# A fp32 encoder block on one core: 256-byte place of the split weights, and the down projection's operands made in steps

## The chip, the cores and the metric

The kernel runs on one core of one Trainium2 chip. The metric is the device time of one execution in microseconds (us). TensorE (PE) multiplies, VectorE (DVE) and ScalarE (ACT) work on tiles in SBUF and PSUM, GpSimd (POOL) issues some transfers, and SyncE (SP) issues most of them.

## The reference

One layer of a bidirectional encoder: 512 tokens, model width 2048, float32 throughout.

```python
h = rmsnorm(x, attn_norm_g);  z = h @ w_in          # [q latent | kv latent | rope key | conv B | C | H]
attn   = attention(8 heads, 128 + 64 rope, no mask)  # from the latents
y_conv = gate_b * conv3_centred(gate_c * sc_h, sc_conv_w)
x = x + concat(rmsnorm(attn), rmsnorm(y_conv)) @ w_o
h = rmsnorm(x, ffn_norm_g)
u = conv3_centred(h @ w_ffn_up, ffn_conv_w) + ffn_conv_b   # 2048 -> 2 x 5632
g, val = split(u);  x = x + (silu(g) * val) @ w_ffn_down   # 5632 -> 2048
return rmsnorm(x, final_norm_g)
```

## The kernel before

**How float32 is kept.** Every float32 operand is split into two tiles of a shorter type: `hi` is a copy by ACT (`split`, L234), `lo` is the difference `src - hi` by DVE (L231, the body of `tt`). A product is then three matmuls, `whi*xhi`, `whi*xlo`, `wlo*xhi` (`mm3` and `product`). Weights come in units of 128x1024 float32 (`raw`, 8 buffers, pool `wraw`, loaded by SP at L261), and each unit is split into a `hi` and a `lo` tile (3 buffers each, pool `wsp`, 4096 bytes in a partition). All other tiles (activations, their halves, sums) are `t` tiles of 128x512 (pool `tp`, 80 buffers, 2048 bytes in a partition); all `t` tiles have the same place modulo 256 bytes. The pools lie one behind the other in the order in which they are made: `cpool`, `tp`, `sp`, `wraw`, `wsp`. In the program as built the `t` tiles begin at 160 modulo 256 bytes and the `hi` and `lo` tiles at 96, which is 192 past the `t` tiles.

**The stages.** Input projections, attention, output projection, the first six tiles of the up projection (`up_plain`) multiply with 512 moving columns at L244 (`mm`). From the seventh of the 44 up tiles on (`up_seven`), and in the down projection (`down_seven`), a 2x2 block product is made by seven products instead of eight (`seven`): 24 matmuls of 256 moving columns for each product (`product`, L880), in the order f1, g7, h6, f2, h5, g4, h3 of PSUM bank and product. Copies by ACT at L936, L957, L969 and L931 take the banks over. One up tile is 7 products, one block of the down projection also 7 (168 matmuls). The down projection runs over five chunks of eight up tiles and in each over four blocks `m`; a last chunk of four tiles runs with plain products of 256 columns at L244 (`last_half`).

**Operands of the down projection.** `gated` saves each activation tile to DRAM through POOL (L782). `sums_of(c, i)` brings two of them back through SP (`restore`, L787) and makes of them the operands of the seven products (`make_operands`): on DVE two differences of 256 columns, two `scalar_tensor_tensor` of 256 columns (L845, L846), one `lo` of 256 and three of 512; on ACT one cast of 256 and three of 512. `fetch_xr` brings 16 tiles of x back in 32 transfers (L1005).

**What sets the order.** The kernel writes a list of items, one for each product; `run` loads weights three or four items ahead, splits them two or three ahead, issues an item's matmuls, and then its `posts` (functions with a lag in items). Over that a scheduler of the framework reorders instructions across engines when the program is built. Each engine then runs its own queue in order, and waits where an input or a buffer isn't free. `sums_of` of chunk 0 stands whole at four of the last up tile's seven items; that of chunk c+1 stands whole on the third item of each block of chunk c.

Of the kernel before, what the change touches and what calls it, by code (L numbers as in the profile page):

```python
# [47 lines left out]
KD = D // P  # L51
# [9 lines left out]
NF = FF // P  # L61
EPS = 1e-6
SCALE = float(1.0 / np.sqrt(np.float32(NOPE + ROPE)))
UW = 1024
NT = 80
NPLAIN = 6
ORDER = [0, 1, 2, 3, 4]
EARLY = ()
AHEAD = 4
HT = T // 2  # L70
FILL = 3
# [100 lines left out]
def encoder_block(ctx: ExitStack, tc: tile.TileContext, gx, wall, vecs, rot, out):  # L172
    nc = tc.nc
    cpool = ctx.enter_context(tc.tile_pool(name="cpool", bufs=1))
    tp = ctx.enter_context(tc.tile_pool(name="tp", bufs=NT))
    sp = ctx.enter_context(tc.tile_pool(name="sp", bufs=2))
    wraw = ctx.enter_context(tc.tile_pool(name="wraw", bufs=8))
    wsp = ctx.enter_context(tc.tile_pool(name="wsp", bufs=3))
    dram = ctx.enter_context(tc.tile_pool(name="dram", bufs=1, space=bass.MemoryType.DRAM))
# [2 lines left out]
    def tile_r():  # L182
        return tp.tile([P, T], F32R, tag="t", name="t")

    def pair():
        return tile_r(), tile_r()

    def ztile():
        return tp.tile([P, T], F32, tag="t", name="t")
# [13 lines left out]
    first = cpool.tile([P, KD + T], F32, name="first")  # L203
    ga = first[:, :KD]
    vec = cpool.tile([P, NVEC], F32, name="vec")
    nvec = cpool.tile([P, 3 * NF], F32, name="nvec")
    cs = []


# [53 lines left out]

    def split_unit(key, part, raw):
        n = part.stop - part.start
        hi = wsp.tile([P, UW], F32R, tag="hi", name="hi")
        lo = wsp.tile([P, UW], F32R, tag="lo", name="lo")
        if key[0] == "kr":

            r = raw.rearrange("p (k c) -> p k c", c=ROPE)  # L270
            w = [z.rearrange("p (k c) -> p k c", c=P) for z in (hi, lo)]
            for j in range(2):
                split((w[j][:, :, :ROPE], w[j][:, :, ROPE:]), r[:, 8 * j:8 * j + 8, :])
            return w
# [48 lines left out]
    items = []  # L323
# [221 lines left out]
    v, qr, qk, pr = {}, {}, {}, {}  # L545
# [227 lines left out]
    def half(t, i):  # L773
        return t[:, i * HT:(i + 1) * HT]
# [3 lines left out]
    def save(name, src):  # L778

        saved[name] = [(dram.tile([P, T], F32, name=f"{name[0]}{name[1]}_{i}"), t.dtype) for i, t in enumerate(src)]  # L780
        for (o, _), t in zip(saved[name], src):
            nc.gpsimd.dma_start(o, t.bitcast(F32))  # L782

    def restore(name):
        ts = [tp.tile([P, T], dt, tag="t", name="t") for _, dt in saved[name]]
        for o, (d, _) in zip(ts, saved[name]):
            nc.sync.dma_start(o.bitcast(F32), d)  # L787
        return ts
# [6 lines left out]
        if s == 0:  # L795
            nc.scalar.activation(u, u, AF.Silu)

    kept = {}

    def gated(us, f):  # L800
        tt(us[1], us[0], us[1], ALU.mult)
        if f // 8 in EARLY:
            kept[f] = us[1]
            if f % 2:
                save(("sums", f // 2), make_operands(kept.pop(f - 1), kept.pop(f)))
            return
        if f < starts[last]:
            save(("act", f), [us[1]])
            return
        a = pair()  # L810
        split(a, us[1])
        save(("act", f), a)
# [19 lines left out]
    operands = []  # L832

    def normed_operands(i):
        (a,), (b,) = restore(("xr", 2 * i)), restore(("xr", 2 * i + 1))
        for k, t in ((2 * i, a), (2 * i + 1, b)):
            nc.vector.scalar_tensor_tensor(out=t, in0=t, scalar=col("ffn_g", k), in1=rx.r, op0=ALU.mult, op1=ALU.mult)
        operands.append(views(make_operands(a, b)))

    def make_operands(a, b):  # L840

        u, v = ztile(), ztile()
        tt(half(u, 0), half(a, 0), half(a, 1), ALU.subtract)
        tt(half(u, 1), half(b, 1), half(a, 1), ALU.subtract)
        nc.vector.scalar_tensor_tensor(out=half(v, 0), in0=half(a, 0), scalar=-1.0, in1=half(u, 1), op0=ALU.mult, op1=ALU.subtract)  # L845
        nc.vector.scalar_tensor_tensor(out=half(v, 1), in0=half(v, 0), scalar=-1.0, in1=half(b, 0), op0=ALU.mult, op1=ALU.subtract)  # L846
        one = tile_r()
        split((half(one, 0), half(one, 1)), half(a, 0))
        ts = [one]
        for src in (u, v, b):  # L850
            p = pair()
            split(p, src)
            ts += p
        return ts

    def views(ts):

        got = {1: (half(ts[0], 0), half(ts[0], 1))}
        for i, names in enumerate(((5, 7), (6, 4), (2, 3))):
            for j, q in enumerate(names):  # L860
                got[q] = half(ts[1 + 2 * i], j), half(ts[2 + 2 * i], j)
        return got

    banks = []
# [18 lines left out]
    def seven(index, units, posts, ops, wide=HT, lean=False):  # L883


        z, raw = {}, {}
# [6 lines left out]
            return f  # L893

        def parts(src):
            hi = wsp.tile([P, UW], F32R, tag="hi", name="hi")
            lo = wsp.tile([P, UW], F32R, tag="lo", name="lo")
            split((hi, lo), src)
            return hi, lo

# [41 lines left out]
        kept, kept2 = [() if a in posts else (a,) for a in ("s7", "u2")]  # L942
# [35 lines left out]
    starts = [sum(CHUNKS[:i]) for i in range(len(CHUNKS))]  # L978
    last = len(CHUNKS) - 1
# [10 lines left out]
    items.extend(plain)  # L990
    for f in range(NPLAIN, NF):
        items.extend(up_seven(f))


    acts, xt, sums = {}, {}, {}
# [9 lines left out]
                    nc.sync.dma_start(half(xt[m, a, h], e), half(saved[("xr", 4 * m + 2 * e + a)][0][0], h))  # L1005

    def sums_of(c, i):
        f = starts[c] + 2 * i
        if c in EARLY:
            ts = restore(("sums", f // 2))  # L1010
        else:
            (a,), (b,) = (restore(("act", f + j)) for j in range(2))
            ts = make_operands(a, b)
        sums.setdefault(c, []).append(views(ts))

    def down_seven(c, m):
        def onto(a, h, op):
# [7 lines left out]
        return seven(m, units, posts, sums.setdefault(c, []), T, True)  # L1025

    at = len(items) - 7
    for i, j in enumerate((0, 2, 4, 5)):
        items[at + j].posts.append((0, lambda i=i: sums_of(ORDER[0], i)))
    for m in range(KD // 4):  # L1030
        items[at + (5, 6, 6, 6)[m]].posts.append((0, lambda m=m: fetch_xr(m)))
    for c, after in zip(ORDER, ORDER[1:] + [None]):
        for m in range(KD // 4):
            its = down_seven(c, m)
            if after is not None:
                its[2].posts.append((0, lambda c=after, m=m: sums_of(c, m)))
            items.extend(its)

    def fetch(f):
# [99 lines left out]
```

## Time and profile before

| | us |
|---|---|
| median of 3 runs | 2034.42 |
| lowest, highest | 2032.77, 2034.82 |
| profiled execution, its own time | 2035.79 |
| span of its instructions | 2034.0 |
| PE busy | 1997.3 (98%) |
| DVE busy | 1542.0 (76%) |
| ACT busy | 977.4 (48%) |

The mean granted clock of PE is 0.992. In a row of a group stand line, engine, operation, output and inputs, shapes, count, then busy time and the mean of one in ns. Matmuls overlap (each starts before the one ahead has drained), so that the mean of one is longer than the distance from start to start; the pace of a stream is read from starts, or from a count in a window. In a row of the timeline stand start, duration of the row, engine, line, operation, and in brackets the idle time ahead of it with what ended it.

### The profile page before, as it was taken

The numbers are of one execution on the slowest core, as the hardware profiler recorded it, in microseconds if no ns is written. First come the engines' busy times: TensorE is split into PE (matmuls) and PEld (weight loads), VectorE is DVE, ScalarE is ACT, GpSimd is POOL, SyncE is SP. The second block draws the span as 40 slices with busy tenths as digits, with TensorE's granted clock in tenths as the row PEclk, the third lists the DMA queues.
The fourth block names the chain that finished last, engine by engine and source line by source line (L and its number), as shares of the span: only waits on it lengthen the run. The fifth ranks groups of instructions, "written<-read, shape, count | busy, mean of one in ns | idle before, by whom it ended". The sixth has DMA issues, their size and how long they took to land.

```text
span 2034.0 us, 33864 instructions
## 1 busy us (share of the span) xinstructions
PE 1997.3 (98%) x13826; PEld 1848.2 (91%) x13826; DVE 1542.0 (76%) x1893; ACT 977.4 (48%) x1358; POOL 209.6 (10%) x204
## 2 busy tenths in 40 slices
PE   8999999999999999999999999999997999999997
PEld 7888888888888888999999999999997999999997
DVE  7375877664556587788888888888887998987776
ACT  6253534433224344555555555555565554444454
POOL 5001232310001000000000000000010001000000
PEclk9999999999999999999999999999998999999998
DMA  7322222222444344445545545545557776677642
GB/s 259 100 86 78 78 78 73 73 91 95 133 138 140 130 156 138 136 134 152 171 136 151 170 137 150 172 138 148 170 143 219 225 197 172 186 187 199 179 116 83
DMA packets 94155, 290.78 MB, mean 143 GB/s; under 512 B 10672, under 2 KB 18992, under 8 KB 94000
## 3 DMA queue, kind: packets, MB, share of 16 engines
q1 hardware_dynamic: 77648, 230.95, 33.9%
q0 software_dynamic: 16352, 57.68, 13.7%
q8 instruction: 108, 1.77, 0.4%
q14 instruction: 47, 0.39, 0.1%
HBM read 267.62 MB, written 20.97 MB: 142 GB/s over the span
## 4 chain that ended last, share of the span: by engine, by line
PE 90%; DVE 4%; DMA 2%; issue 1%; ACT 0%; SPq 0%; DVEq 0%; ACTq 0%
PE ps L880 50%; PE ps L244 41%; DVE t L231 2%; DMA t<-act 2%; DVE lo L231 2%; DVE raw L231 0%; ACT hi L234 0%; DVE t L846 0%; SPq L787 0%; DVE t L845 0%; SPq L261 0%; DVE t L489 0%; DVEq L1134 0%; ACT ps L931 0%; ACT t L349 0%
## 5 line engine op out<-in xcount | busy, mean ns | idle before, releaser
L880 PE MATMUL ps<-t,hi 128*128 128x256 f32 x6496 | 1118.5, 278 | 17.7 <-ACT hi L234 7.2
L880 PEld LDWEIGHTS ps<-t,hi 128*128 128x128 f32 x6496 | 978.1, 188 | 20.3 <-DVE t L231 8.0
L234 ACT CAST hi<-raw 128x1024 fp32r<-128x1024 f32 (+1 forms) x544 | 568.3, 1047 | 702.9 <-PE ps L244 242.3
L880 PE MATMUL ps<-t,lo 128*128 128x256 f32 x3248 | 884.4, 278 | 1.9 <-DVE lo L231 1.9
L231 DVE TENSOR_TENSOR lo<-raw,hi 128x1024 fp32r<-128x1024 f32 (+1 forms) x543 | 668.4, 1232 | 198.4 <-ACT hi L234 188.3
L244 PE MATMUL ps<-t,hi 128*128 128x512 f32 x2096 | 654.3, 394 | 4.4 <-ACT t L239 3.5
L880 PEld LDWEIGHTS ps<-t,lo 128*128 128x128 f32 x3248 | 602.8, 188 | 2.6 <-DVE lo L231 2.5
L244 PEld LDWEIGHTS ps<-t,hi 128*128 128x128 f32 x2096 | 394.3, 189 | 92.0 <-ACT t L239 4.2
L244 PE MATMUL ps<-t,lo 128*128 128x512 f32 x1056 | 411.4, 392 | 0.0
L231 DVE TENSOR_TENSOR t<-ps,t 128x512 f32<-128x512 f32 (+3 forms) x255 | 143.0, 575 | 152.6 <-PE ps L244 99.8
L231 DVE TENSOR_TENSOR t<-t 128x512 fp32r<-128x512 f32 (+4 forms) x356 | 223.1, 645 | 34.2 <-DMA t<-act 13.2
L244 PEld LDWEIGHTS ps<-t,lo 128*128 128x128 f32 x1056 | 198.9, 188 | 45.0 <-issue 0.5
L231 DVE TENSOR_TENSOR raw<-raw 128x1024 f32<-128x1024 f32 x154 | 187.8, 1219 | 0.5
L244 PE MATMUL ps<-t 128*128 128x256 f32 (+1 forms) x642 | 108.6, 326 | 0.0
L234 ACT CAST t<-t 128x512 fp32r<-128x512 f32 (+2 forms) x149 | 81.3, 577 | 48.8 <-DVE t L231 25.1
L244 PEld LDWEIGHTS ps<-t 128*128 128x128 f32 x642 | 95.1, 190 | 10.3
L231 DVE TENSOR_TENSOR t<-t,ps 128x512 f32<-128x512 f32 x128 | 86.7, 683 | 21.1 <-PE ps L880 19.7
L782 POOL DMA_DIRECT2D act<-t x48 | 27.4, 570 | 694.4 <-DVE t L231 658.9
L231 POOL TENSOR_TENSOR t<-t 128x512 f32<-128x512 f32 x39 | 64.1, 1645 | 72.3 <-DVE t L231 40.5
L904 POOL DMA_DIRECT2D raw<-wall x58 | 50.3, 868 | 163.6 <-ACT t L936 69.4
L910 POOL DMA_DIRECT2D raw<-wall x20 | 17.1, 854 | 316.8 <-DVE lo L231 215.5
L343 ACT ACTIVATE t<-l 128x512 f32<-128x512 f32 x44 | 27.5, 626 | 45.7 <-DVE l L231 45.5
(81 smaller groups left out, 825.3 us busy)
## 6 DMA issues: line engine op xcount, KB each, us to landing
raw<-wall SPq DMA_DIRECT2D x372, 512.0 KB, 4.3
raw<-wall POOLq DMA_DIRECT2D x78, 512.0 KB, 7.4
act<-t POOLq DMA_DIRECT2D x48, 256.0 KB, 2.5
t<-act SPq DMA_DIRECT2D x48, 256.0 KB, 5.1
t<-gx SPq DMA_DIRECT2D x16, 256.0 KB, 3.8
xr<-l POOLq DMA_DIRECT2D x16, 256.0 KB, 2.4
t<-xr SPq DMA_DIRECT2D x16, 256.0 KB, 4.0
t<-xr SPq DMA_DIRECT2D x32, 128.0 KB, 3.9
```

What stands on the lines that cost most here:

```text
L231: (eng or nc.vector).tensor_tensor(out=o, in0=a, in1=b, op=op)
L234: nc.scalar.copy(out=dst[0], in_=src)
L244: nc.tensor.matmul(ps, lhsT=w, rhs=x, start=start, stop=stop)
L343: nc.scalar.activation(sq, src, AF.Square)
L782: nc.gpsimd.dma_start(o, t.bitcast(F32))
L880: nc.tensor.matmul(half(ps, e), lhsT=w[a][:, c:c + P], rhs=ops[k][q][b], start=start and e == k == i == 0, stop=k == n - 1 and i == 2, ski ...
L904: nc.gpsimd.dma_start(raw["a21"], wall[UIDX[units["a22"]]], accum_op=ALU.add)
L910: nc.gpsimd.dma_start(raw["s"], wall[UIDX[units["a12"]]], accum_op=ALU.add)
```

## The change

Two things, beside the removal of code that does nothing here (`ORDER`, `EARLY`, `kept`, `views`).

The first is **addresses**. The `hi` and `lo` buffers grow by 64 floats (`ROOM`). Weights for 512 columns (`split_unit`) use the start of the buffer; weights for 256 columns (`parts` in `seven`) start 48 floats, which is 192 bytes, behind it. The pool `sp` is made ahead of `tp`, and the small table `nvec` lies in a part of `first` that the input's first tile no longer needs, and not in a tile of its own. In the program as built the `t` tiles and the `hi` and `lo` buffers then all begin at 64 modulo 256 bytes: 512-column weights lie 0 past the tiles (before 192), 256-column weights 192 past them (as before). The one product that uses `t` tiles as weights and `hi`, `lo` as 256 moving columns (`values` in the attention, 192 matmuls) goes from a distance of 64 to 0.

The second is **steps**. `sums_of` now returns five functions: a fetch of two tiles, and four steps of the making of operands. For chunk 0 they are posted from eight items ahead of the last up tile's first on, to its last; for later chunks on the items 0, 2, 3, 4, 5 of a block.

```diff
+ROOM = 64
+SHIFT = 48
...
+    sp = ctx.enter_context(tc.tile_pool(name="sp", bufs=2))
     tp = ctx.enter_context(tc.tile_pool(name="tp", bufs=NT))
-    sp = ctx.enter_context(tc.tile_pool(name="sp", bufs=2))
...
-    nvec = cpool.tile([P, 3 * NF], F32, name="nvec")
+    nvec = first[:, KD:KD + 3 * NF]
...
     def split_unit(key, part, raw):
-        hi = wsp.tile([P, UW], F32R, tag="hi", name="hi")
-        lo = wsp.tile([P, UW], F32R, tag="lo", name="lo")
+        hi, lo = (wsp.tile([P, UW + ROOM], F32R, tag=a, name=a)[:, :UW] for a in ("hi", "lo"))
...
         def parts(src):
-            hi = wsp.tile([P, UW], F32R, tag="hi", name="hi")
-            lo = wsp.tile([P, UW], F32R, tag="lo", name="lo")
+            hi, lo = (wsp.tile([P, UW + ROOM], F32R, tag=a, name=a)[:, SHIFT:SHIFT + UW] for a in ("hi", "lo"))
...
+    def operand_steps(a, b, got):
+        z = {}
+        def parts(src, *names):
+            p = pair()
+            split(p, src)
+            for j, q in enumerate(names):
+                got[q] = half(p[0], j), half(p[1], j)
+        def first():
+            z["u"], one = ztile(), tile_r()
+            tt(half(z["u"], 0), half(a(), 0), half(a(), 1), ALU.subtract)
+            tt(half(z["u"], 1), half(b(), 1), half(a(), 1), ALU.subtract)
+            got[1] = half(one, 0), half(one, 1)
+            split(got[1], half(a(), 0))
+        def second():
+            v = z["v"] = ztile()
+            nc.vector.scalar_tensor_tensor(out=half(v, 0), in0=half(a(), 0), scalar=-1.0, in1=half(z["u"], 1), op0=ALU.mult, op1=ALU.subtract)
+            nc.vector.scalar_tensor_tensor(out=half(v, 1), in0=half(v, 0), scalar=-1.0, in1=half(b(), 0), op0=ALU.mult, op1=ALU.subtract)
+            parts(z["u"], 5, 7)
+        return first, second, lambda: parts(z["v"], 6, 4), lambda: parts(b(), 2, 3)
...
     def sums_of(c, i):
-        f = starts[c] + 2 * i
-        if c in EARLY:
-            ts = restore(("sums", f // 2))
-        else:
-            (a,), (b,) = (restore(("act", f + j)) for j in range(2))
-            ts = make_operands(a, b)
-        sums.setdefault(c, []).append(views(ts))
+        z, f = {}, starts[c] + 2 * i
+        got = {}
+        sums.setdefault(c, []).append(got)
+        def fetch2():
+            for j in range(2):
+                (z[j],) = restore(("act", f + j))
+        return fetch2, *operand_steps(lambda: z[0], lambda: z[1], got)
...
-    for i, j in enumerate((0, 2, 4, 5)):
-        items[at + j].posts.append((0, lambda i=i: sums_of(ORDER[0], i)))
+    for i, when in enumerate(((-8, -6, -5, -4, -3), (-1, 1, 1, 2, 3), (1, 4, 4, 5, 5), (3, 4, 5, 6, 6))):
+        for j, step in zip(when, sums_of(0, i)):
+            items[at + j].posts.append((0, step))
...
-            if after is not None:
-                its[2].posts.append((0, lambda c=after, m=m: sums_of(c, m)))
+            if c + 1 < last:
+                for j, step in zip((0, 2, 3, 4, 5), sums_of(c + 1, m)):
+                    its[j].posts.append((0, step))
```

In the program as built the queues differ only from the second to last up tile to the fourth block of the down projection; in later blocks single rows of 128x256 change places. Three places there follow.

**SP's queue at the end of the up projection.** `raw` are weight loads, `act` the fetches of activations in pairs. Before:

```order
L261 DMA raw<-wall 128x1024 x151
L787 DMA t<-act_0_5498 128x512
L787 DMA t<-act_0_5690 128x512
L261 DMA raw<-wall 128x1024 x2
L787 DMA t<-act_0_5882 128x512
L787 DMA t<-act_0_6047 128x512
L261 DMA raw<-wall 128x1024
L787 DMA t<-act_0_6311 128x512
L787 DMA t<-act_0_6389 128x512
```

and after:

```order
L264 DMA raw<-wall 128x1024 x147
L789 DMA t<-act_0_5497 128x512
L789 DMA t<-act_0_5689 128x512
L264 DMA raw<-wall 128x1024 x3
L789 DMA t<-act_0_5881 128x512
L789 DMA t<-act_0_6046 128x512
L264 DMA raw<-wall 128x1024 x2
L789 DMA t<-act_0_6310 128x512
L789 DMA t<-act_0_6388 128x512
```

The first pair stands four weight loads earlier, the second three, the third two; the fourth pair, not shown, stands one earlier.

**DVE's queue in the second to last up tile.** Rows of 128x1024 are weights (`lo`, or sums of `raw`), rows of 128x512 belong to the saved activation, rows of 128x256 to the operands. Before:

```order
L231 TENSOR_TENSOR t_14746<-t_14780,t_14746 128x512
L231 TENSOR_TENSOR lo_14854<-raw_14576,hi_14853 128x1024
L231 TENSOR_TENSOR raw_14948<-raw_14814,raw_14816 128x1024
L231 TENSOR_TENSOR t_14820<-t_14746,t_14819 128x512
L231 TENSOR_TENSOR lo_14886<-raw_14617,hi_14885 128x1024
L231 TENSOR_TENSOR lo_14919<-raw_14708,hi_14918 128x1024
```

and after:

```order
L234 TENSOR_TENSOR t_14745<-t_14783,t_14745 128x512
L234 TENSOR_TENSOR lo_14863<-raw_14575,hi_14862 128x1024
L234 TENSOR_TENSOR raw_14972<-raw_14817,raw_14819 128x1024
L234 TENSOR_TENSOR t_14823<-t_14745,t_14822 128x512
L234 TENSOR_TENSOR t_14856<-t_14773 128x256
L234 TENSOR_TENSOR t_14856<-t_14775,t_14773 128x256
L234 TENSOR_TENSOR lo_14902<-raw_14616,hi_14901 128x1024
L234 TENSOR_TENSOR t_14857<-t_14773,t_14857 128x256
L855 SCALAR_TENSOR_TENSOR t_14894<-t_14773,t_14856 128x256
L234 TENSOR_TENSOR lo_14939<-raw_14707,hi_14938 128x1024
```

The first pair's differences now stand ahead of a weight's `lo`. On PE the product of `lo_14902` now goes ahead of that of `lo_14863`; in before the product of `lo_14854` went ahead of that of `lo_14886`.

**ACT's queue ahead of the last up tile's seventh product.** `hi` are weights, `t<-t` casts of operands, `t<-ps` the copy that empties the PSUM bank of the sixth product's place for the next one. Before:

```order
L234 CAST hi_15208<-raw_14948 128x1024
L234 CAST t_15067<-t_15055 128x512
L234 CAST t_15071<-t_15052 128x512
L234 CAST t_15084<-t_14986 128x512
L936 COPY t_15124<-ps_15093 128x256
L234 CAST t_15160<-t_15150 128x256
```

and after:

```order
L237 CAST hi_15215<-raw_14972 128x1024
L237 CAST t_15130<-t_15121 128x512
L938 COPY t_15144<-ps_15096 128x256
L237 CAST t_15170<-t_15127 128x512
L938 COPY t_15180<-ps_6303 128x256
```

One cast stands between the weight's `hi` and the copy where three stood.

## Rows read from the trace of the kernel before

**Rows 1.** The page: busy share of PE, and the chain by line.

```profile
PE 1997.3 (98%) x13826; PEld 1848.2 (91%) x13826; DVE 1542.0 (76%) x1893; ACT 977.4 (48%) x1358; POOL 209.6 (10%) x204
PE ps L880 50%; PE ps L244 41%; DVE t L231 2%; DMA t<-act 2%; DVE lo L231 2%; DVE raw L231 0%; ACT hi L234 0%; DVE t L846 0%; SPq L787 0%; DVE t L845 0%; SPq L261 0%; DVE t L489 0%; DVEq L1134 0%; ACT ps L931 0%; ACT t L349 0%
```

**Rows 2.** The page's groups of matmuls: shapes, count, busy us, mean ns.

```profile
L880 PE MATMUL ps<-t,hi 128*128 128x256 f32 x6496 | 1118.5, 278 | 17.7 <-ACT hi L234 7.2
...
L880 PE MATMUL ps<-t,lo 128*128 128x256 f32 x3248 | 884.4, 278 | 1.9 <-DVE lo L231 1.9
...
L244 PE MATMUL ps<-t,hi 128*128 128x512 f32 x2096 | 654.3, 394 | 4.4 <-ACT t L239 3.5
...
L244 PE MATMUL ps<-t,lo 128*128 128x512 f32 x1056 | 411.4, 392 | 0.0
```

**Rows 3.** Timeline of PE, 190 to 216 us: split weights, attention, split weights.

```profile
189.69 0.39 PE L244 MATMUL ps<-t,lo 128*128 128x512 f32 x1
...
197.47 7.41 PE L244 MATMUL ps<-t 128*128 128x512 f32 x32
204.72 0.62 PE L244 MATMUL ps<-t,hi 128*128 128x512 f32 x2
...
215.02 0.62 PE L244 MATMUL ps<-t,hi 128*128 128x512 f32 x2
```

**Rows 4.** Windows: stretch, its us, busy us (count) by engine, PE's clock, DMA.

```profile
900.00:1500.00 600.00, 600.00 (x5297) 600.00 (x5296) 497.02 (x538) 347.28 (x475) 44.46 (x62) 1.00 0.52 152
1540.99:1572.45 31.46, 19.41 (x122) 17.90 (x121) 22.49 (x38) 14.50 (x26) 2.85 (x4) 0.78 0.80 249
...
1845.00:1975.00 130.00, 130.00 (x1108) 130.00 (x1108) 102.33 (x115) 59.41 (x73) 9.92 (x12) 1.00 0.62 163
1979.00:2001.00 22.00, 22.00 (x186) 22.00 (x185) 12.50 (x30) 12.15 (x30) 0.00 (x0) 1.00 0.01 2
```

**Rows 5.** Groups of 256-column matmuls at L244, shapes kept apart.

```profile
L244 PE MATMUL ps<-t 128*128 128x256 f32 x384 | 47.8, 284 | 0.0
L244 PE MATMUL ps<-hi,t 128*128 128x256 f32 x128 | 22.7, 278 | 0.0
```

**Rows 6.** Timeline of PE around the first blocks of the down projection.

```profile
1521.97 0.62 PE L880 MATMUL ps<-t,hi 128*128 128x256 f32 x4
...
1544.54 0.79 PE L880 MATMUL ps<-t,hi 128*128 128x256 f32 x2 [3.37 <-ACT t L936]
...
1555.87 1.58 PE L880 MATMUL ps<-t,hi 128*128 128x256 f32 x4 [6.96 <-ACT hi L234]
...
1642.34 0.50 PE L880 MATMUL ps<-t,hi 128*128 128x256 f32 x2 [1.39 <-DVE t L231]
```

**Rows 7.** Timeline of ACT, 1541 to 1552 us.

```profile
1541.14 1.04 ACT L234 CAST hi<-raw 128x1024 fp32r<-128x1024 f32 x1 [1.44 <-PE ps L880]
1542.56 1.66 ACT L234 CAST t<-t 128x512 fp32r<-128x512 f32 x3 [0.38 <-DVE t L846]
1544.13 0.36 ACT L936 COPY t<-ps 128x256 f32<-128x256 f32 x1
1551.43 0.41 ACT L234 CAST t<-t 128x256 fp32r<-128x256 f32 x1 [6.93 <-DMA t<-act]
```

**Rows 8.** Timeline of DVE, at 1521 us and from 1634 us.

```profile
1521.35 1.22 DVE L231 TENSOR_TENSOR lo<-raw,hi 128x1024 fp32r<-128x1024 f32 x1
...
1633.98 1.22 DVE L231 TENSOR_TENSOR lo<-raw,hi 128x1024 fp32r<-128x1024 f32 x1
1635.12 0.42 DVE L846 SCALAR_TENSOR_TENSOR t<-t 128x256 f32<-128x256 f32 x1
1635.46 0.68 DVE L231 TENSOR_TENSOR t<-t,ps 128x512 f32<-128x512 f32 x1
1636.05 1.22 DVE L231 TENSOR_TENSOR lo<-raw,hi 128x1024 fp32r<-128x1024 f32 x1
```

**Rows 9.** The page: fetches of activations, count, KB each, us to landing.

```profile
t<-act SPq DMA_DIRECT2D x48, 256.0 KB, 5.1
```

More of the change, by code (lines that the diff above doesn't have):

```diff
@@ L65 @@
 NT = 80
+ROOM = 64
+SHIFT = 48
 NPLAIN = 6
-ORDER = [0, 1, 2, 3, 4]
-EARLY = ()
 AHEAD = 4
@@ L796, in conv_up @@
             nc.scalar.activation(u, u, AF.Silu)
-    kept = {}
     def gated(us, f):
         tt(us[1], us[0], us[1], ALU.mult)
[L802 to L806, printed above, removed]
         if f < starts[last]:
@@ L837, in normed_operands, with make_operands @@
             nc.vector.scalar_tensor_tensor(out=t, in0=t, scalar=col("ffn_g", k), in1=rx.r, op0=ALU.mult, op1=ALU.mult)
[L838 to L850, printed above, removed]
+        operands.append(make_operands(a, b))
+    def operand_steps(a, b, got):
+        z = {}
+        def parts(src, *names):
             p = pair()
             split(p, src)
[L853 to L859, printed above, removed]
-            for j, q in enumerate(names):
-                got[q] = half(ts[1 + 2 * i], j), half(ts[2 + 2 * i], j)
+            for j, q in enumerate(names):
+                got[q] = half(p[0], j), half(p[1], j)
[11 more added lines that the diff above has]
+        return first, second, lambda: parts(z["v"], 6, 4), lambda: parts(b(), 2, 3)
+    def make_operands(a, b):
+        got = {}
+        for step in operand_steps(lambda: a, lambda: b, got):
+            step()
         return got
@@ L1007, in sums_of @@
     def sums_of(c, i):
-        f = starts[c] + 2 * i
-        if c in EARLY:
-            ts = restore(("sums", f // 2))
-        else:
-            (a,), (b,) = (restore(("act", f + j)) for j in range(2))
-            ts = make_operands(a, b)
-        sums.setdefault(c, []).append(views(ts))
+        z, f = {}, starts[c] + 2 * i
+        got = {}
+        sums.setdefault(c, []).append(got)
[3 more added lines that the diff above has]
+        return fetch2, *operand_steps(lambda: z[0], lambda: z[1], got)
     def down_seven(c, m):
@@ L1027, in encoder_block @@
     at = len(items) - 7
-    for i, j in enumerate((0, 2, 4, 5)):
-        items[at + j].posts.append((0, lambda i=i: sums_of(ORDER[0], i)))
+    for i, when in enumerate(((-8, -6, -5, -4, -3), (-1, 1, 1, 2, 3), (1, 4, 4, 5, 5), (3, 4, 5, 6, 6))):
+        for j, step in zip(when, sums_of(0, i)):
+            items[at + j].posts.append((0, step))
     for m in range(KD // 4):
         items[at + (5, 6, 6, 6)[m]].posts.append((0, lambda m=m: fetch_xr(m)))
-    for c, after in zip(ORDER, ORDER[1:] + [None]):
+    for c in range(last):
         for m in range(KD // 4):
             its = down_seven(c, m)
-            if after is not None:
-                its[2].posts.append((0, lambda c=after, m=m: sums_of(c, m)))
+            if c + 1 < last:
+                for j, step in zip((0, 2, 3, 4, 5), sums_of(c + 1, m)):
+                    its[j].posts.append((0, step))
             items.extend(its)
```

## The prediction

> **What bounds the kernel now.** I read the page first: PE is busy for 98% of the span, and 91% of the chain that ended last is PE at two lines, L880 and L244 [rows 1]. So there are two ways to gain: a shorter distance from one matmul to the next, and fewer holes between them. The groups give the counts, 3152 matmuls of 512 columns with split weights and 9744 of 256 columns [rows 2].
>
> For the pace I read starts in the timeline. Around one attention block PE changes from weights in `hi` and `lo` buffers to weights in `t` tiles and back: the 32 matmuls of `t` by `t` take 204.72 - 197.47 = 7.25 us, 226.6 ns each; the 45 split ones behind them take 215.02 - 204.72 = 10.30 us, 228.9 ns each, and the 34 ahead of them 7.78 us, 228.8 ns each [rows 3]. Shapes and the full clock are the same, so 2.3 ns depends on what the operands are or where they lie. `t` by `t` lies 0 apart modulo 256 bytes, the split weights 192.
>
> With 256 columns there are three levels. The up stage holds 600 us / 5297 = 113.3 ns; the down stage behind its last holes 130 / 1108 = 117.3 ns; the last stage (`t` by `t`, 0 apart) 22 / 186 = 118.3 ns, all at a clock of 1.00 [rows 4]. The by-form groups say the same of the last: 284 ns as mean of one, against 278 for `values`, which has `t` weights and `hi`, `lo` moving [rows 5]. So 0 apart looks best for 512 columns and worst for 256.
>
> The holes I read last. Between 1540.99 and 1572.45 us PE runs 122 matmuls, which at 113.3 ns are 13.8 us of the 31.5; 17.6 us are lost, and the clock is 0.78, part of the stretch at 1.2 GHz instead of 2.4 [rows 4]. Two holes carry most: 3.4 us until ACT's copy at L936, and 7.0 us until a weight's `hi` [rows 6]. Behind them four holes of the kind at 1642.34 us are left, 1.4 us of waiting each for a DVE sum that empties a PSUM bank [rows 6].
>
> **The change part by part.**
>
> *512 columns.* The weights move from 192 past the moving tiles to 0, the distance of `t` by `t`. At that stream's pace the gain is 3152 x 2.3 ns = **-7.2 us**. Nothing hides it: in these stages PE has next to no idle time (4.4 us in the whole `hi` group, [rows 2]). The ends are 0, if the place isn't the cause, and -8. I take -7.2, since it is the same engine, shape and clock seconds apart.
> The Trainium skill speaks against this in "TensorE: Matmul & The Clock Gate", section "Step-by-step: what each phase is for": TensorE's two read ports into SBUF are independent, one for the moving operand and one for weights, so that loading weights takes nothing from a running matmul. By that rule a distance between the two addresses costs nothing, and this term would be 0. The step from 226.6 to 228.9 ns doesn't follow from that rule, though it doesn't refute it either, as long as no run moves the addresses alone.
>
> *256 columns at L880.* Their distance stays 192, so their pace stays: 0. *`values`.* 192 matmuls go from 64 apart to 0, which is the distance of the group with 284 against 278 ns [rows 5]: 192 x about 5.5 ns = **+1.0 us** (ends -0.3 and +1.2). *`nvec`* keeps its place on DVE, early on, and waits for the same transfer: 0.
>
> *The end of the up projection.* In before, chunk 0's operands come late and in a lump. The first hole: ACT ran three casts of operands in 1.66 us, after waiting 0.38 us for DVE's L846, ahead of the copy that PE wanted [rows 7]. The second: ACT stood 6.93 us for a fetch [rows 7], with the next weight's `hi` queued behind it, and a fetch needs 5.1 us from issue to landing [rows 9]. Now the four fetches are posted 8, 3, 3 and 2 items earlier, an item being 24 x 113.3 ns = 2.7 us: 22, 8, 8 and 5 us; in SP's queue that is four, three, two and one weight loads earlier. The second hole came of the second pair, and 8 us cover the 6.93: it goes. The third and fourth pair, 8 and 5 us earlier, land about when they are wanted, and leave small waits.
>
> What is late next I price by walking the new queues with durations of the trace: a `lo` keeps DVE 1635.12 - 1633.98 = 1.14 us, an operation of 256 columns 0.34, one of 512 0.59 [rows 8]; a `hi` keeps ACT 1.0 us and a cast of 512 some 0.55 [rows 7].
> - In the second to last up tile two differences (0.68 us) now stand ahead of a `lo`, which in before began at 1521.35 [rows 8]: it ends at 1521.35 + 0.68 + 1.14 = 1523.17. PE now wants it for the third matmul of the product that starts at 1521.97 [rows 6], at 1522.20: a new hole of 1.0 us.
> - Ahead of the seventh product of the last up tile ACT runs a `hi` that has to wait for PE to end the product before, then one cast, then the copy: 1.0 + 0.55 + 0.36, about 2.0 us of hole where there were 3.4. The copies and casts queued behind it move by the same.
> - Seven smaller ones in the same way, 0.25 us in that last tile and 0.10, 0.45, 0.90, 0.35, 0.40 and 0.75 around the third and fourth pair: 3.2 us.
>
> Together 6.2 us of holes. From the first on I take the pace of the down stage: some 335 matmuls up to the second block x 4.0 ns = 1.3 us. Lost are then 7.5 us instead of 17.6: **-10.1 us**. Bounds: if one long wait stays and the clock falls to 1.2 GHz again, 13 to 14 us stay lost, -4; if nearly all new holes are covered by work that the scheduler left ahead of PE, -17. I stay between, at the walk, since each of its steps is priced by a row of the same queue and stretch.
>
> *Later blocks.* Of the four holes of 1.4 us the first nearly goes (-1.3 us), since the making of operands no longer stands whole ahead of that sum; of the other three, and one smaller, the order takes one 256-column operation out of DVE's queue ahead of the sum, 0.34 us each [rows 8]: **-2.6 us** together (ends 0 and -6, if all go). Nothing else moves there: DVE's work is the same.
>
> *Sum.* -7.2 + 1.0 - 10.1 - 2.6 = -18.9 us. The profiled execution takes 2035.79 us, its span 2034.0; -18.9 gives 2016.9. The median lies 1.4 us below that execution, so 2034.4 - 18.9 = **2015.5 us**.
>
> **Rivals.**
> - *The up stage takes the slower level* (slower than before). 256 columns show 113.3 or 117.3 ns at one and the same distance [rows 4], so the distance alone doesn't set the level: the rhythm in which PE enters does. The up stage has 38 tiles x 168 = 6384 matmuls; entered at 117.3 they take 25.5 us more, 2041 us. What decides is the first `up_seven`, behind 512-column matmuls whose rhythm this change alters. For it: the down stage stays at the slower level once holes have come. Against: the up stage has no hole, and holds its level for 600 us. 9%.
> - *The place does nothing* (the change doesn't do what it says): 226.6 ns belongs to `t` by `t` for another reason, such as three matmuls on one weight tile's two parts. Then -7.2 and +1.0 fall away: 2021.7 us. This is also what the rule on the ports gives. Against it is that both column counts step with the distance. 12%.
> - *The operands stay late:* the clock falls again, only 4 us are won there: 2021.6 us. For it: between 1541 and 1572 us the clock was 0.78 [rows 4], and two new holes come within 20 us. 10%.
> - *Without long holes the down stage keeps 113.3 ns:* 3360 matmuls x 4.0 ns = 13.4 us less, 2002 us; kept for half of the stage, 2009. Against: small holes are left, and any hole may change the level. 9%.
>
> **How the numbers follow.** Forecast 57%, place without effect 12%, late operands 10%, faster level 9%, slower level 9%; 3% for a way that ends where before ended. The forecast's own bounds are 2009 to 2022 (transition at -4 or -17). The range 2004 to 2024 takes in late operands, place without effect and the half-kept faster level, and leaves out the slower level and part of the faster. A measurement here tells 0.2%, 4 us, from no change: faster 0.88, same 0.03, slower 0.09.
>
> **What would show it.** Right: `t` weights and split weights at L244 alike near 226.6 ns; about 2 to 3 ns more per matmul of `values`; no wait of PE over 2.5 us from 1500 to 1600 us, a clock near 1.00 there, and no ACT row that waits 6.9 us for a fetch; the up stage still 5297 in 600 us. Wrong: 228.9 ns kept (first term gone), a count near 5115 in 600 us (slower level), or a wait on a fetch in the last up tile.

## The result, and the profile after

The changed kernel takes 2048.6 us (2047.7 to 2050.64, 4 runs) against 2034.38 us of the kernel before in the same comparison: a ratio of 1.0072, with a 95% interval of 1.0056 to 1.0088. It is slower by 0.7%. The forecast was 2015.5 us, with a range that ended at 2024. What came is the rival to which it gave 9%.

The page of the changed kernel, busy shares and the chain by line (lines are three or so further down than before: L883 is `product`, L247 is `mm`):

```profile
PE 2018.8 (99%) x13826; PEld 1875.1 (92%) x13826; DVE 1543.0 (75%) x1893; ACT 975.9 (48%) x1358; POOL 209.1 (10%) x204
...
PE ps L883 46%; PE ps L247 40%; DMA t<-act 1%; DVE t L234 1%; DVE lo L234 0%; DMA raw<-wall 0%; DMA t<-xr 0%; POOL raw L906 0%; ACT hi L237 0%; DVE raw L234 0%; DVE t L855 0%; SPq L1007 0%; POOL act L784 0%; DVE t L856 0%; POOL raw L912 0%
```

PE is busy for 21.5 us more than before [rows 1] with the same 13826 matmuls, while the shares of DVE and of fetches on the chain have shrunk. The groups of matmuls say which ones got dearer:

```profile
L883 PE MATMUL ps<-t,hi 128*128 128x256 f32 x6496 | 1145.1, 280 | 9.4 <-DVE t L234 3.9
L883 PE MATMUL ps<-t,lo 128*128 128x256 f32 x3248 | 892.3, 280 | 1.3 <-DVE lo L234 1.2
L247 PE MATMUL ps<-t,hi 128*128 128x512 f32 x2096 | 649.4, 392 | 5.0 <-ACT t L242 4.3
L247 PE MATMUL ps<-t,lo 128*128 128x512 f32 x1056 | 409.4, 390 | 0.0
```

Against [rows 2], 512 columns cost 2 ns less each, 256 columns 2 ns more, and the idle time ahead of the first group fell from 17.7 to 9.4 us. The windows show where (first the output projection, then the up stage, the change to the down stage, and the down stage):

```profile
500.00:600.00 100.00, 100.00 (x445) 82.56 (x444) 52.70 (x69) 26.07 (x30) 0.00 (x0) 1.00 0.41 136
900.00:1500.00 600.00, 600.00 (x5097) 600.00 (x5096) 480.80 (x518) 333.03 (x457) 43.02 (x60) 1.00 0.49 145
1500.00:1600.00 100.00, 95.53 (x784) 93.90 (x784) 86.56 (x113) 56.93 (x83) 9.14 (x13) 0.98 0.69 208
...
1850.00:1950.00 100.00, 100.00 (x851) 99.98 (x850) 76.27 (x80) 42.10 (x45) 8.52 (x10) 1.00 0.67 179
```

The up stage runs 5097 matmuls in 600 us where it ran 5297 [rows 4]: 117.7 ns instead of 113.3, with PE busy all the time, at a clock of 1.00, and without a hole. (A window also counts the matmuls that its edges cut, so that a pace from a count comes out a little short: by starts it is 117.8.) The place where it begins, before and after:

```profile
825.42 0.39 PE L244 MATMUL ps<-t,lo 128*128 128x512 f32 x1
825.65 0.39 PE L880 MATMUL ps<-t,hi 128*128 128x256 f32 x2
825.88 0.28 PE L880 MATMUL ps<-t,lo 128*128 128x256 f32 x1
825.99 0.39 PE L880 MATMUL ps<-t,hi 128*128 128x256 f32 x2
```

```profile
820.50 0.39 PE L247 MATMUL ps<-t,lo 128*128 128x512 f32 x1
820.72 0.40 PE L883 MATMUL ps<-t,hi 128*128 128x256 f32 x2
820.96 0.28 PE L883 MATMUL ps<-t,lo 128*128 128x256 f32 x1
821.07 0.40 PE L883 MATMUL ps<-t,hi 128*128 128x256 f32 x2
```

The first three matmuls of 256 columns take 0.34 us before and 0.35 after: the level is there from the first one on. The stream begins 4.9 us earlier, which is the gain with 512 columns, and then loses 4.4 ns with each matmul.

The end of the up projection went nearly as it was meant to:

```profile
1567.16 0.50 PE L883 MATMUL ps<-t,hi 128*128 128x256 f32 x2 [1.86 <-ACT t L938]
1575.94 0.39 PE L883 MATMUL ps<-t,hi 128*128 128x256 f32 x1 [0.29 <-ACT t L237]
1576.88 0.62 PE L883 MATMUL ps<-t,hi 128*128 128x256 f32 x3 [0.56 <-ACT hi L237]
```

```profile
1575.48 0.41 ACT L237 CAST t<-t 128x256 fp32r<-128x256 f32 x1 [1.65 <-DMA t<-act]
```

No wait of PE is longer than 1.9 us, where there were 3.4 and 7.0 [rows 6], and ACT waits 1.65 us for a fetch where it waited 6.93 [rows 7]. The clock of 1500 to 1600 us is 0.98 and not 1.00, for it still fell once, 1 us after the end of the wait of 1.86 us:

```profile
1568.20:1571.40 3.20, 3.20 (x17) 3.20 (x16) 2.42 (x5) 1.41 (x3) 0.00 (x0) 0.50 0.96 224
```

At 0.50, which is 1.2 GHz, 15 matmuls started some 214 ns apart instead of 118: an estimate of 1.5 us lost from these starts. In the kernel before it fell twice there (0.78 in [rows 4]).

Both traces have the same 13826 matmuls, so the start of the n-th in one can be set against the start of the n-th in the other. By that, the difference of 13.4 us between the spans is made up of:

| stretch | forecast, us | measured, us |
|---|---|---|
| up to the first 256-column product | -6.2 | -4.9 |
| up stage to the first hole, 6145 matmuls | 0 | +27.3 |
| from there to the second block of the down projection | -10.1 | -8.8 |
| later blocks | -2.6 | -0.4 |
| last stage | 0 | +0.1 |

The first row moves from one execution to the next: in the traces of the other runs with these addresses, described below, the first 256-column product, or the extra matmuls ahead of it, comes 2.7 to 6.2 us earlier than in before.

### The profile page after: what moved, and what is told of

It is laid out like the page before. It is cut to its first block, busy times and chain, and to the rows that moved or that the text cites. A ratio compares the mean times of both kernels' runs of the same rounds, so it can differ in the third digit from the quotient of the medians.

```text
span 2047.4 us, 33861 instructions
## 1 busy us (share of the span) xinstructions
PE 2018.8 (99%) x13826; PEld 1875.1 (92%) x13826; DVE 1543.0 (75%) x1893; ACT 975.9 (48%) x1358; POOL 209.1 (10%) x204
## 4 chain that ended last, share of the span: by engine, by line
PE 86%; issue 8%; DMA 1%; DVE 1%; POOL 0%; ACT 0%; SPq 0%; DVEq 0%; POOLq 0%; ACTq 0%
PE ps L883 46%; PE ps L247 40%; DMA t<-act 1%; DVE t L234 1%; DVE lo L234 0%; DMA raw<-wall 0%; DMA t<-xr 0%; POOL raw L906 0%; ACT hi L237 0%; DVE raw L234 0%; DVE t L855 0%; SPq L1007 0%; POOL act L784 0%; DVE t L856 0%; POOL raw L912 0%
## 5 line engine op out<-in xcount | busy, mean ns | idle before, releaser
L883 PE MATMUL ps<-t,hi 128*128 128x256 f32 x6496 | 1145.1, 280 | 9.4 <-DVE t L234 3.9
L883 PEld LDWEIGHTS ps<-t,hi 128*128 128x128 f32 x6496 | 986.4, 188 | 12.6 <-DVE t L234 5.3
L883 PE MATMUL ps<-t,lo 128*128 128x256 f32 x3248 | 892.3, 280 | 1.3 <-DVE lo L234 1.2
L247 PE MATMUL ps<-t,hi 128*128 128x512 f32 x2096 | 649.4, 392 | 5.0 <-ACT t L242 4.3
L883 PEld LDWEIGHTS ps<-t,lo 128*128 128x128 f32 x3248 | 602.9, 188 | 2.2 <-DVE lo L234 2.1
L247 PEld LDWEIGHTS ps<-t,hi 128*128 128x128 f32 x2096 | 393.9, 188 | 89.4 <-ACT t L242 5.1
L247 PE MATMUL ps<-t,lo 128*128 128x512 f32 x1056 | 409.4, 390 | 0.0
L247 PEld LDWEIGHTS ps<-t,lo 128*128 128x128 f32 x1056 | 198.8, 188 | 42.2 <-issue 0.5
L247 PE MATMUL ps<-t 128*128 128x256 f32 (+1 forms) x642 | 108.5, 326 | 0.0
L247 PEld LDWEIGHTS ps<-t 128*128 128x128 f32 x642 | 95.1, 190 | 10.1
```

The costliest lines, as they stand in the source:

```text
L247: nc.tensor.matmul(ps, lhsT=w, rhs=x, start=start, stop=stop)
L883: nc.tensor.matmul(half(ps, e), lhsT=w[a][:, c:c + P], rhs=ops[k][q][b], start=start and e == k == i == 0, stop=k == n - 1 and i == 2, ski ...
```

## The experiments

The theories. **E**: the level of the 256-column pace is set by what PE does as it enters the stream, and is kept until something disturbs it. **A**: it belongs to the absolute addresses. **S**: the steps set it. For the small remainder, theories on the later blocks follow at e9.

**e1: steps alone.** The addresses of before, the order of the changed kernel, as an edit of the changed kernel (lines with a minus are the changed kernel's).

```diff
-    sp = ctx.enter_context(tc.tile_pool(name="sp", bufs=2))
     tp = ctx.enter_context(tc.tile_pool(name="tp", bufs=NT))
+    sp = ctx.enter_context(tc.tile_pool(name="sp", bufs=2))
...
-    nvec = first[:, KD:KD + 3 * NF]
+    nvec = cpool.tile([P, 3 * NF], F32, name="nvec")
...
-        hi, lo = (wsp.tile([P, UW + ROOM], F32R, tag=a, name=a)[:, :UW] for a in ("hi", "lo"))
+        hi, lo = (wsp.tile([P, UW], F32R, tag=a, name=a) for a in ("hi", "lo"))
...
-            hi, lo = (wsp.tile([P, UW + ROOM], F32R, tag=a, name=a)[:, SHIFT:SHIFT + UW] for a in ("hi", "lo"))
+            hi, lo = (wsp.tile([P, UW], F32R, tag=a, name=a) for a in ("hi", "lo"))
```

> The changed kernel's order (the operands of the down projection in steps), with the addresses of the kernel before: split weights 192 bytes past the tiles modulo 256 for 512 and for 256 columns. Theory E (the entry: the pace of 256 columns is set by the stream that PE comes from, and kept until a hole): the 512-column stream runs at 228.9 ns as before, so the up stage is entered as before and runs at 113.3 ns from 825 us on; only the end of the up projection changes, by about -10 us: about 2024 us. Theory S (the steps set the slower pace of the up stage): 117.8 ns in the up stage, about 2053 us. Theory A (absolute addresses set it) gives the same as E here.

2029.19 us against 2033.59, a ratio of 0.9973 (0.9962 to 0.9984). The up stage:

```profile
900.00:1500.00 600.00, 600.00 (x5296) 600.00 (x5295) 496.61 (x539) 347.25 (x474) 44.48 (x62) 1.00 0.52 152
```

Theory S falls. The end of the up projection gave 8.2 us by the start of the same matmul, and the later blocks took 2.4 back, so that the steps alone gained some 4 us and not 10.

**e2: addresses alone.** The kernel before with `ROOM`, `SHIFT`, the pools and `nvec` of the changed one.

> The addresses of the changed kernel with the order of the kernel before, row by row on all five engines. Theories E and A: 512 columns at 226.7 ns (-5 us by the first 256-column product), then the up stage at 117.8 ns (+28 us), then the late operands as before: about 2057 us. Theory S: -5 us only, about 2029 us.

2056.67 us, a ratio of 1.011 (1.0095 to 1.0125). The up stage:

```profile
900.00:1500.00 600.00, 600.00 (x5097) 600.00 (x5096) 480.81 (x518) 332.99 (x458) 43.04 (x60) 1.00 0.48 145
```

The whole loss comes with the addresses. In this trace the down stage went over to 113 ns behind some of its holes, with nothing else about it changed, for some 1400 matmuls in all; one such stretch:

```profile
1863.00:1950.00 87.00, 87.00 (x770) 87.00 (x770) 69.26 (x72) 36.60 (x38) 7.64 (x9) 1.00 0.68 182
```

So the level isn't a property of the stage either. The trace of e5 has it too, for some 1400 matmuls, and in both runs the traced execution is the fastest of the four, by 4 us. That is about what 1400 matmuls at 4.4 ns less give (6 us, an estimate), so the level behind a hole seems to differ from one execution to the next; the other executions have no trace that would show it.

**e3: both kinds 192 past the tiles.** In `split_unit`:

```diff
-        hi, lo = (wsp.tile([P, UW + ROOM], F32R, tag=a, name=a)[:, :UW] for a in ("hi", "lo"))
+        hi, lo = (wsp.tile([P, UW + ROOM], F32R, tag=a, name=a)[:, SHIFT:SHIFT + UW] for a in ("hi", "lo"))
```

> The changed kernel with the 512-column weights moved 192 bytes up too, so that both kinds lie 192 past the tiles, as in the kernel before, but at other absolute places (tiles at 64, weights at 0 modulo 256; before 160 and 96). Theory E: 512 columns at 228.9 ns, the up stage is entered as before and runs at 113.3 ns: 2048.6 + 5 - 29 = about 2025 us. Theory A: 117.8 ns in the up stage whatever the 512-column stream does: about 2054 us.

2028.11 us, one run. The output projection and the up stage:

```profile
500.00:600.00 100.00, 100.00 (x440) 81.86 (x440) 51.59 (x69) 26.00 (x30) 0.00 (x0) 1.00 0.40 137
900.00:1500.00 600.00, 600.00 (x5297) 600.00 (x5295) 496.52 (x539) 346.79 (x474) 44.55 (x62) 1.00 0.52 152
```

Theory A falls: the 256-column weights and all tiles lie where they lie in the changed kernel, to the byte, and the stage runs at 113.3 ns. Only the 512-column weights ahead of it have moved. And 512 columns at 440 instead of 445 in 100 us show that their distance costs what the forecast said.

**e4: both kinds at distance 0.** `SHIFT = 0`.

> The changed kernel with the 256-column weights at distance 0 from the tiles too. If distance 0 gives the pace of tiles by tiles, 256 columns run at 120.0 ns in both stages, with no second level: 9744 x (120.0 - 117.8) = 21 us more than the changed kernel, about 2070 us. If there are two levels here too, or if the distance doesn't matter, the up stage shows 113.3 or 117.8 ns.

2066.72 us, one run. The up stage:

```profile
900.00:1500.00 600.00, 600.00 (x5002) 600.00 (x5002) 471.57 (x507) 323.66 (x447) 43.10 (x60) 1.00 0.48 143
```

120.0 ns, one level. So the distance decides which levels there are, 120.0 ns alone at 0, 113.3 and 117.8 at 192; at 192 something else decides between the two. The Trainium skill ("TensorE: Matmul & The Clock Gate", section "Step-by-step: what each phase is for") has loading weights take nothing from a running matmul, since TensorE reads weights and moving data through two independent ports. e3 and e4 moved nothing but the place of weights, and the pace moved by 2.2 ns each. By that rule it should not have moved; here the measurement decides. Whether the time is lost at the ports no run shows.

**e5 and e6: the last 512-column unit alone.** Of the changed kernel, and of e3, only the last 24 matmuls ahead of the up stage change their distance. In `split_unit`, for e5 (e6 has the two values exchanged):

```diff
+        o = SHIFT if key == ("up", 1, NPLAIN - 1, 1) else 0
-        hi, lo = (wsp.tile([P, UW + ROOM], F32R, tag=a, name=a)[:, :UW] for a in ("hi", "lo"))
+        hi, lo = (wsp.tile([P, UW + ROOM], F32R, tag=a, name=a)[:, o:o + UW] for a in ("hi", "lo"))
```

> The changed kernel, with only one 512-column unit, the last ahead of the first product of 256 columns (24 matmuls), moved 192 bytes up; all other 512-column units stay at distance 0; order the same on all engines. Theory E (what PE does just ahead of the first product sets the level, and it holds until a hole): 24 matmuls at 228.9 ns (+0.06 us), then the up stage at 113.3 ns: 2048.6 - 28.5 = about 2020 us. Theory L (the long stream or something earlier sets it, not the last matmuls): 117.8 ns in the up stage, 2048.6 us.

> The opposite: all weights 192 past the tiles, but for that one last 512-column unit, which lies at distance 0; order the same. Theory E: the stream at 228.9 ns as in the kernel before, its last 24 matmuls at 226.7 ns, then the up stage at 117.8 ns: about 2028 + 28 = 2056 us. Theory L: 113.3 ns, 2028 us.

e5 took 2048.42 us, a ratio of 1.0075 (1.0058 to 1.0091); e6 2054.59 us, one run. e6 is what theory E said: 24 matmuls out of some 3700 turn the level of the 6145 that follow up to the first hole. e5 is not: its last 24 matmuls had the pace of before and yet the slow level followed. The records of the starts, in ns from one matmul to the next, tell why. First the last six of 512 columns, then extra ones, then the first six of the product, then the mean of the next 1200:

```
before   226 229 232 226 229 232                113 113 114 113 113 114   113.3
e3       226 229 232 226 229 232                113 113 114 113 113 114   113.3
e5       229 231 226 229 232 226                117 119 117 118 118 118   117.8
after    227 227 226 227 227 226                117 118 118 117 119 117   117.8
e6       227 226 227 227 226 226                118 118 117 118 118 118   117.8
e7       226 227 227 226 227 227  113 119 120..  113 114 113 113 114 113   113.3
e8       226 227 227 226 227 227  113 119 121    113 114 113 113 114 113   113.3
```

At distance 192 the 512-column stream has a rhythm of three, 226, 229, 232. In before it ends with 232, in e5, where it began 24 matmuls ago from another stream, with 226. So the pace of the last stream alone doesn't decide. The point of its rhythm at which the product comes in fits all seven rows, though no run moves that point and nothing else. Theory E holds in that narrower sense, and theory L, which gave e5's time, fails in e6.

**e7 and e8: a few matmuls ahead of the first product.** The changed kernel with 12 (e7) and 3 (e8) matmuls of 256 columns, tiles by tiles, into the bank that the product then overwrites. In `seven`:

```diff
-                product(bank_of(name, start), w, q, start, ops)
+                ps = bank_of(name, start)
+                if wide == HT and index == NPLAIN and q == 1:
+                    for _ in range(KICK):
+                        mm(half(ps, 0), h2[0][0][:, :P], half(h2[0][0], 0), True, True)
+                product(ps, w, q, start, ops)
```

> The changed kernel with 12 extra matmuls of 256 columns, tiles by tiles (distance 0), ahead of the first product, into a bank that the product then overwrites. They should run at 120 ns and cost 1.4 us. In the trace of the kernel before, 256-column products that followed such matmuls ran at 113.3 ns in the last stage. Theory E: the level is set anew, and if it falls as there, 113.3 ns: 2048.6 + 1.4 - 28.5 = about 2021.5 us. If the level belongs to the addresses of this kernel after a 512-column stage, however entered: 117.8 ns, 2050 us.

> The changed kernel with 3 extra matmuls of 256 columns, tiles by tiles, ahead of the first product, instead of 12. Theory E, with the rhythm of the few matmuls just ahead as what counts: the second and third already ran 119 and 120 ns apart when there were 12, so 3 are enough: up stage at 113.3 ns, 0.4 us for the three, about 2022 us. If three are too few to leave the rhythm of the 512-column stream: 117.8 ns, 2049 us.

e7 took 2023.49 us (one run), e8 2023.75 us, a ratio of 0.9943 (0.9925 to 0.996) to the kernel before: 25 us less than the changed kernel for three matmuls that take 0.35 us. Its rows:

```profile
822.74 0.39 PE L248 MATMUL ps<-t,lo 128*128 128x512 f32 x1
822.97 0.52 PE L248 MATMUL ps<-t 128*128 128x256 f32 x3
823.32 0.39 PE L884 MATMUL ps<-t,hi 128*128 128x256 f32 x2
...
823.66 0.39 PE L884 MATMUL ps<-t,hi 128*128 128x256 f32 x2
```

The loss was the entry, and e8 beats both kernels, the one before by 0.6%.

**e9: the later blocks.** In the changed kernel's later blocks ACT waits ten times as long for fetches. ACT's waits from 1590 to 1860 us, before and after (what waited, for what: us in total, times, longest):

```profile
ACT t L234 <- DMA t<-act: 2.0, 2, 1.3
```

```profile
ACT t L237 <- DMA t<-act: 20.3, 7, 4.7
```

The cast of the first operand needs only the fetch, and the first step lets it stand on ACT ahead of weights' casts. e9 is e8 with that split in the second step (`operand_steps`):

```diff
         def first():
-            z["u"], one = ztile(), tile_r()
+            z["u"] = ztile()
             ...
-            got[1] = half(one, 0), half(one, 1)
-            split(got[1], half(a(), 0))
         def second():
             ...
+            one = tile_r()
+            got[1] = half(one, 0), half(one, 1)
+            split(got[1], half(a(), 0))
             parts(z["u"], 5, 7)
```

> As e8, and the split of the first operand (one cast of 256 columns on ACT, one operation on DVE) goes from the first step into the second, behind the two scalar_tensor_tensor as in the kernel before. In the later blocks of the down projection the cast then stands on ACT behind two weight casts and behind the copy L933, no longer ahead of them. Theory W (the 2.6 us forecast for later blocks didn't come because this cast now waits for the fetch with weights behind it: ACT waits 20 us for DMA t<-act there, before none): that wait falls to a few us and the kernel takes 1 to 3 us less than e8. Theory D (DVE's own wait for the fetch, 7 to 9 us, is what PE feels): no difference over 0.5 us.

2024.92 us, a ratio of 0.9958 (0.9942 to 0.9974). The wait in question from 1570 to 1860 us, in e8 and in e9:

```profile
ACT t L238 <- DMA t<-act: 19.2, 7, 4.1
```

```profile
ACT t L238 <- DMA t<-act: 7.8, 3, 3.9
```

It fell as theory W said, and the time did not. But the edit moved more than that wait. PE's own waits from 1570 to 1860 us, in e8 and in e9 (the copy at L938 of e8 and L939 of e9 is L933 of the changed kernel):

```profile
PE ps L884 <- DVE t L235: 3.8, 4, 1.3
PE ps L884 <- ACT hi L238: 1.3, 3, 0.4
PE ps L884 <- ACT ps L938: 0.2, 1, 0.2
```

```profile
PE ps L885 <- DVE t L235: 4.0, 4, 1.4
PE ps L885 <- ACT ps L939: 1.3, 2, 0.7
PE ps L885 <- ACT hi L238: 0.4, 1, 0.4
PE ps L885 <- DVE lo L235: 0.2, 1, 0.2
```

The waits for a weight's `hi`, which stands behind the late cast, fell from 1.3 to 0.4 us, and the others rose from 4.0 to 5.5. The edit also acts at the end of the up projection, where PE's wait for the copy that is L938 in the changed kernel grew from 1.9 to 4.5 us. So PE seems to have felt ACT's wait by some 0.9 us, and the later place of the cast cost as much or more elsewhere: W's gain of 1 to 3 us didn't come, but its cause is neither shown nor excluded. A time that stays the same within some us fits D too; that DVE's wait is the cause isn't shown by it.

**e10 and e11: can the level be set anywhere?** e10 is e8 with three more such matmuls ahead of the first product of the fourth block of chunk 3 in the down stage (`again` is true there).

```diff
+                if again and q == 1:
+                    for _ in range(KICK):
+                        mm(half(ps, 0), ops[1][1][0][:, :P], ops[0][1][0], True, True)
```

> As e8 (3 tile-by-tile matmuls ahead of the first product of the up stage), with 3 more ahead of the first product of the fourth block of chunk 3 of the down projection, behind the last hole of that stage in all traces so far; orders on the other four engines as in e8. Theory E: the level can be set anew anywhere by what PE does just ahead, also in the down stage, with the same addresses: some 720 matmuls from there to the last stage run at 113.3 instead of 117.8 ns, -3.2 us, less 0.4 us for the three: about 2021 us against 2023.8 of e8. If the slower level belongs to the down stage (its busier DVE, ACT or transfers): 117.8 ns stays and it takes 0.4 us more than e8.

2023.37 us, a ratio of 0.9949 (0.9936 to 0.9963). A window of the down stage that begins with the three:

```profile
1850.00:1950.00 100.00, 100.00 (x850) 99.97 (x850) 78.09 (x86) 44.68 (x53) 7.68 (x9) 1.00 0.70 180
```

117.8 ns stayed. Either the down stage keeps it, or three such matmuls don't always do it. e11 reads the level behind 25 groups of extra matmuls of 1 to 12, in both stages (a group that the scheduler parted counts as two):

```diff
+KICKS = {(None, 6): (256, 3), (None, 8): (512, 3), (None, 10): (256, 3), (None, 12): (256, 3), (None, 14): (512, 3),
...
+         (None, 36): (256, 5), (3, 3): (256, 12), (4, 0): (512, 3), (4, 1): (256, 6), (4, 2): (512, 12), (4, 3): (256, 4)}
...
+                if q == 1:
+                    n, times = KICKS.get((chunk, index), (0, 0))
+                    for _ in range(times):
+                        mm(z["full"][:, :n], ops[1]["t"][:, :P], ops[0]["t"][:, :n], True, True)
```

> The changed kernel with extra matmuls, tiles by tiles (distance 0), ahead of the first product of every second up tile, and of the last five blocks of the down projection that have products: 1 to 12 of 256 or 512 columns, in turn. Not a version to be fast: it reads the level after each. Theory R (the rhythm of the few matmuls just ahead decides, whatever the stage and the level before): after each group of 256 columns 113.3 ns, after each group of 512 columns 117.8 ns, in the up stage and in the down stage alike. Theory M (the finer phase decides, which the kind of the matmuls ahead fixes only in part): the same kind gives both levels. If the stage decides: the up stage follows the kind, the down stage stays at 117.8 ns.

2052.82 us, with the extra work. Four of its windows, behind 3 of 256 columns, behind 5 of 512, behind 6 of 256 in the down stage, behind 3 of 512 there:

```profile
890.00:920.00 30.00, 30.00 (x257) 30.00 (x256) 22.37 (x25) 16.42 (x23) 1.44 (x2) 1.00 0.58 168
1372.00:1400.00 28.00, 28.00 (x249) 28.00 (x249) 22.71 (x26) 16.58 (x22) 1.44 (x2) 1.00 0.45 141
1912.00:1929.00 17.00, 17.00 (x152) 17.00 (x151) 12.05 (x13) 6.69 (x7) 1.05 (x2) 1.00 0.63 167
1941.00:1952.00 11.00, 11.00 (x96) 11.00 (x95) 7.70 (x10) 3.65 (x5) 0.00 (x0) 1.00 0.48 159
```

249 in 28 us and 152 in 17 us are the fast level, 257 in 30 and 96 in 11 the slow one (two or three of each count are matmuls that the edges cut). All groups, but for one that met a hole:

| the stream ahead of the group | 256 columns: of so many, fast after | 512 columns: of so many, fast after |
|---|---|---|
| 512 columns, distance 0 | 1 of 1 (with e7 to e10: 5 of 5) | none |
| fast level | 3 of 3 | 1 of 4 |
| slow level | 2 of 9 | 1 of 7 |

The stage doesn't decide: the down stage was at 113.3 ns behind six matmuls at 1910 us. Nor does the kind of matmul alone. Of the three, theory M is what is left: the level follows from the point in the rhythm at which the product begins, for which the stream ahead of the group counts too. That is a reading of these rows and not a test. Out of the 512-column stream or the fast level the extra matmuls of 256 columns settled at 120 ns, and the fast level followed each time; out of the slow level they mostly ran unevenly, 115 to 124 ns, and the slow level mostly came back.

## Why the prediction was wrong

- **What bounds the kernel** was read rightly: pace and holes of PE, with the clock behind a hole, make up the whole difference.
- **512 columns** (-7.2 with +1.0 for `values`): right in cause, since e3 moves the weights alone. The matmuls' pace fell from 228.9 to between 226.7 and 227.3 ns by stretch, 2.1 ns in the mean and not 2.3. 4.9 us came of the 6.2; some 0.5 us are a later start of the first matmuls in this one execution. `values` cost the 1.0 us, by starts 114.8 ns before and 119.9 after; in the rows 278 [rows 5] and now 283:

```profile
L247 PE MATMUL ps<-hi,t 128*128 128x256 f32 x128 | 23.7, 283 | 0.0
```

  The sign named for it, 2 to 3 ns more per matmul, didn't fit the 5.5 ns of its own sum.
- **256 columns at L880: "Their distance stays 192, so their pace stays: 0"**: this is the step that failed. The distance fixes a pair of levels, and the entry chooses. It measured +27.3 us, in e2 too. The section's own rows had both levels at one distance [rows 4], and the rival on the slower level drew that conclusion and named what decides ("the first `up_seven`, behind 512-column matmuls whose rhythm this change alters"); its price of 25.5 us was short, since the slower level is 117.8 ns by starts, and the window that gave 117.3 took in the start of the last stage. (The 118.3 ns of that stage is likewise a mean: its steady stretches run at 120.) The 9% was the mistake: that the up stage has no hole was counted against it, and that says only that the level is kept, not which one is entered. The trace had no entry from a 512-column stream at distance 0, so that nothing in it said which level would follow.
- **The end of the up projection** (-10.1): right in mechanism, with the holes nearly where they were walked: 1.9 us ahead of L938 where 2.0 was expected, and small ones at the third and fourth pair. The new hole of 1.0 us was half as long, and with the up stage at 113.3 ns, in e1, it is 1.1. What the sum put at nothing, and only its bounds had, is the clock: it fell once more behind the wait of 1.9 us and took an estimated 1.5 us. Measured -8.8; e1 alone -8.2.
- **Later blocks** (-2.6): mis-sized. The holes for the DVE sum shrank as forecast: of the four of 1.4 us the first is all but gone, and the other three are 1.06. But new ones, which the sum put at nothing, came behind ACT, three of some 0.45 us behind a weight's `hi` and one of 0.98 behind a copy:

```profile
1653.35 0.51 PE L883 MATMUL ps<-t,hi 128*128 128x256 f32 x2 [1.06 <-DVE t L234]
1668.39 0.50 PE L883 MATMUL ps<-t,hi 128*128 128x256 f32 x2 [0.45 <-ACT hi L237]
...
1833.26 0.50 PE L883 MATMUL ps<-t,hi 128*128 128x256 f32 x2 [0.98 <-ACT ps L933]
```

  They ate most of it: -0.4 in the changed kernel, and +2.4 in e1. What makes ACT late there stays open; its longer wait for fetches seems to have a part in the `hi` holes (e9).
- **Rivals.** That the place does nothing falls (e3, e4). That the down stage might keep the fast level didn't come in the changed kernel; parts of the stage had it in e2, e5 and e7. Without the entry's loss the sum would have held better, though not wholly: e8, 2023.75 us, lies just inside the range, 8 us above the forecast.
- **What would show it** was right and enough: "a count near 5115 in 600 us (slower level)". 5097 were there. The clock near 1.00 that was named for a right forecast was 0.98.

## What to carry to other kernels

Where a stream of matmuls shows two paces in one trace at the same shape, clock and addresses, the pace is a state that is entered; look at what stands ahead of the entry, and price an edit there by the whole stream that follows. An address that is better for one stage can cost more at the border to the next. If the entry is bad, a few cheap matmuls ahead of it may mend it, but only the trace after shows whether they did, since three such matmuls left the level as it was in the down stage (e10).

## What the runs showed of the hardware

The start-to-start time of fp32 split matmuls depends on where weights lie against the moving tile, modulo 256 bytes as far as these places tell: with 512 columns 226.7 ns at 0 and 228.9 at 192; with 256 columns 120.0 at 0, 114.8 at 64 (`values` in the kernel before, where the moving tiles are the split ones), and 113.3 or 117.8 at 192. No run tells a period of 256 bytes from one of 128. In cycles of 2.4 GHz a group of three matmuls takes 816, 848 or 864 with 256 columns, 1632 or 1648 with 512: steps of 16 cycles. The level held for 6300 matmuls and 715 us without a hole, and was set by as few as three matmuls. The entry decided it in e3 and e6 to e8; behind a hole either level can follow. What in the engine or in SBUF makes a rhythm fall into one or the other wasn't found; no run here changes the phase by itself.
